# Eight, eight and six couples by seven products a layer: merged bank evacuation, in-place sums of weights, one ring of split pieces

## The chip, the cores and the metric

The kernel runs on one core of a Trainium2 chip. The metric is the device time of one execution in microseconds. Before the change the median of three runs was 2391.03 us (2389.68 to 2392.11).

## The reference

Two layers on 256 tokens of width 2048. A layer is RMSNorm, a token mixer (layer 0 an mLSTM, layer 1 an HGRN2), a residual, RMSNorm, a gated MLP with a depthwise convolution of width 3 along the tokens, and a residual; a last RMSNorm closes the trunk. The change touches mainly the MLP:

```
u = hn @ w_up                        # 2048 -> 2 x 5504
a, v = split(u)
c = conv_b + sum_j a[t + j - 1] * conv_w[j]
y = (gelu(c) * v) @ w_down           # 5504 -> 2048
```

## The kernel before

**Precision.** Every float32 operand x is used as two parts, a rounded high part (`wh`, made by ScalarE, L137) and the rest (`wl`, made by VectorE as x - wh, L138). A block product is three TensorE matmuls: high by high, high by low, low by high (`product`, L234). Each weight therefore passes through ScalarE and VectorE once. Weights come from HBM into `raw` tiles (three buffers of 128x2048) on the queue of SP, and the split *pieces* of 128x1024 go into a ring of four (`WB`).

**Chunks.** `stream` (L282) walks a list of chunks and stays three pieces ahead of TensorE (`LOOK`). An "fm" chunk gives one feature tile (up projections, queries, keys, gates), a "tm" chunk 512 output columns for the 256 tokens. An up chunk ("fm", `paced`) holds 128 columns of a and 128 of v. They fill two PSUM banks of `psm`; in each bank columns 0 to 255 hold the high sum and 256 to 511 the low one. `done_up` (in `ffn`, L1097 on) evacuates: copy the low half (ScalarE, L355), add (VectorE, L356), scale by the norm (L361), once for a and once for v; then the convolution (VectorE L1118 to L1120), Gelu, the product with v, and the split into the tile `g` (`GT`).

**Parts.** The MLP is done in two parts of 22 and 21 feature tiles. Part 0 is 22 up chunks, then two down *pairs* (output columns 0 to 1023, `w_d0`, and 1024 to 2047, `w_d1`). Part 1 is 21 up chunks, one pair (columns 0 to 1023) and two "tm" chunks for the rest.

**Pairs and couples.** A pair ("st", `squares_by_seven`, L226) takes two feature tiles (a *couple*) at a time, as a 2x2 by 2x2 block product: tokens are two blocks of 128, outputs two blocks of 512. A plain couple takes eight block products into the banks C11, C12, C21, C22 (tile `pc`). A couple listed in `SEVEN` takes seven (Winograd's form) with sums of the token blocks S1 to S4 and sums of the weight blocks T1 to T4, three of the products going into the banks P1, P5, P6, P7 (tile `mm`). `mid` adds these into the residual `hm` (VectorE and GpSimd, L547 to L554) after the last couple by seven, and `done` adds C11 to C22 (L559). In part 0 couples 1, 2, 4, 5, 7, 8, 9 and 1, 2, 4, 5, 7, 8 go by seven in the two pairs, in part 1 couples 1, 2, 4, 5, 7, 8: 19 a layer.

**Sums of weights.** Those of the couples in `STORED` (six a pair) are made while the up chunks run: `prepare` (L573) loads a couple's weights into tiles `pth`, three VectorE subtractions (L179, 182, 184) make the sums in `ptl`, and they go to HBM (`tscr`). `side.push` paces it: its waits are counted in units of TensorE work as emitted, 10.4 a chunk. The pair loads them back into tiles `T` (tag `avc`, three buffers, shared with the up chunks' evacuation). Couple 9 of the first pair makes its sums live. `combine` (L200) splits T into `th0`, `tl0`, `th1`, `tl1`, one buffer each (L209, L210). Sums of tokens are made in `token_sums` (L527) at the end of the odd up chunk.

**Mixers.** Their output projections (`mixed`, L587) hold one such pair of eight couples, three by seven, with sums made live.

**Order.** Instructions of an engine run in the order of a scheduler that plans when the program is built; it may move a matmul of one couple ahead of one of another. Waits are semaphores.

## Time and profile before

| what | value |
|---|---|
| median of three runs | 2391.03 us |
| span of the profiled execution | 2388.5 us (its whole time isn't given) |
| TensorE busy | 2372.4 us (99%), 14614 matmuls |
| VectorE busy | 1944.1 us (81%), 3221 instructions |
| ScalarE busy | 1298.8 us (54%), 2013 instructions |
| GpSimd busy | 189.7 us (8%) |
| moved by DMA | 555 MB, 232 GB/s over the span |

"Busy" of an engine is the time in which at least one of its instructions ran. A row of a group reads: line, engine, operation, output and inputs, shapes, count, then total busy time, mean time of one in ns, and the idle time before them with what ended it. A row of waits reads: who waited for whom, us in total, times, longest. A row of windows gives each engine's busy time in a stretch with its count, the granted clock of TensorE, the DMA engines' busy share and GB/s. A row of the chain or the timeline begins with its start and its length in us.

### The profile page before, as it was taken

Reading aid. Unit: us, or ns where it says so; the run is one execution under the profiler, and the core shown is the slowest. Engines: PE = TensorE matmul, PEld = TensorE weight load, DVE = VectorE, ACT = ScalarE, POOL = GpSimd, SP = SyncE. Lnnn points to the kernel's source line nnn. Section 1 sums busy time; section 2 is a strip of 40 time slices with the busy share of each in tenths; the row PEclk is TensorE's granted clock in tenths of the full one; section 3 lists DMA queues with packets and bytes.
Section 4 is the critical chain, followed back from the end, with each engine's and each line's share of the span. In section 5 each row is a group of like instructions: output and inputs, shape, how many; then the busy total and the mean of one; then the engine's idle time right before and its main releaser. Section 6 shows DMA issues by size and latency. Waiting matters only on the chain.

```text
span 2388.5 us, 37988 instructions
## 1 busy us (share of the span) xinstructions
PE 2372.4 (99%) x14614; PEld 2030.4 (85%) x14614; DVE 1944.1 (81%) x3221; ACT 1298.8 (54%) x2013; POOL 189.7 (8%) x240
## 2 busy tenths in 40 slices
PE   9999999999999999999999999999999999999998
PEld 7888888888888888888888888888888888888887
DVE  7766687988887888777888888888889888788874
ACT  7655455454564554555555555555555565454563
POOL 0100000000000000001222222220000000000000
PEclk9999999999999999999999999999999999999999
DMA  8654556988787777755554554545798888677774
GB/s 300 201 180 165 183 178 211 333 294 317 269 293 254 251 239 262 273 194 182 173 171 168 175 177 160 177 166 188 258 325 298 298 281 296 231 249 263 249 266 148
DMA packets 98789, 555.07 MB, mean 232 GB/s; under 512 B 11168, under 2 KB 11680, under 8 KB 50736
## 3 DMA queue, kind: packets, MB, share of 16 engines
q1 hardware_dynamic: 96912, 548.64, 65.6%
q0 software_dynamic: 1120, 3.21, 0.7%
q8 instruction: 114, 1.87, 0.3%
q10 hardware_dynamic: 576, 0.79, 0.1%
q14 instruction: 67, 0.55, 0.1%
HBM read 512.69 MB, written 39.91 MB: 231 GB/s over the span
## 4 chain that ended last, share of the span: by engine, by line
PE 98%; DVE 1%; issue 1%; DMA 0%; ACT 0%; SPq 0%; POOLq 0%; POOL 0%
PE mm L328 37%; PE mm L344 23%; PE mm L332 18%; PE pc L237 12%; PE mm L237 5%; PE pn L776 1%; PE py L1034 1%; PE pd L984 1%; PE pz L405 0%; PE pa L984 0%; DMA raw<-in_w_first 0%; PE S L762 0%; DVE tl L210 0%; PE pz L1055 0%; PE pa L1009 0%
## 5 line engine op out<-in xcount | busy, mean ns | idle before, releaser
L328 PE MATMUL mm<-xt,wh 128*128 128x512 f32 x3776 | 1313.4, 394 | 0.0
L137 ACT CAST wh<-raw 128x1024 fp32r<-128x1024 f32 (+1 forms) x846 | 853.5, 1019 | 693.8 <-PE mm L328 237.9
L138 DVE TENSOR_TENSOR wl<-raw,wh 128x1024 fp32r<-128x1024 f32 (+1 forms) x846 | 1004.7, 1195 | 265.1 <-ACT wh L137 257.6
L332 PE MATMUL mm<-xt,wl 128*128 128x256 f32 x3776 | 1045.9, 278 | 0.0
L328 PEld LDWEIGHTS mm<-xt,wh 128*128 128x128 f32 x3776 | 706.2, 188 | 159.4
L332 PEld LDWEIGHTS mm<-xt,wl 128*128 128x128 f32 x3776 | 709.5, 188 | 4.5 <-issue 0.4
L344 PE MATMUL mm<-wh,xt 128*128 128x512 f32 x1024 | 320.5, 391 | 3.0 <-ACT xt L350 1.3
L344 PEld LDWEIGHTS mm<-wh,xt 128*128 128x128 f32 x1024 | 191.4, 188 | 43.3 <-ACT xt L350 1.7
L344 PE MATMUL mm<-wl,xt 128*128 128x512 f32 x512 | 198.2, 391 | 0.0
L237 PE MATMUL pc<-wh,g 128*128 128x512 f32 x508 | 167.2, 389 | 0.0
L355 ACT COPY b<-mm 128x256 f32<-128x256 f32 x236 | 87.4, 370 | 122.9 <-PE mm L332 122.7
L210 DVE TENSOR_TENSOR tl<-T,th 128x1024 fp32r<-128x1024 f32 x88 | 109.9, 1264 | 38.9 <-ACT th L209 36.7
L209 ACT CAST th<-T 128x1024 fp32r<-128x1024 f32 x88 | 92.7, 1054 | 73.6 <-PE mm L237 43.5
L237 PEld LDWEIGHTS pc<-wh,g 128*128 128x128 f32 x508 | 95.4, 188 | 19.9
L344 PEld LDWEIGHTS mm<-wl,xt 128*128 128x128 f32 x512 | 96.2, 188 | 18.9
L553 POOL TENSOR_TENSOR hm<-hm,u 128x512 f32<-128x512 f32 x8 | 10.4, 1302 | 1150.9 <-DVE u L552 1150.9
L237 PE MATMUL pc<-wl,g 128*128 128x512 f32 x254 | 98.9, 389 | 0.0
L344 PE MATMUL mm<-wh,g 128*128 128x512 f32 x308 | 96.6, 392 | 0.0
L237 PE MATMUL mm<-th,sx 128*128 128x512 f32 x264 | 91.9, 390 | 0.0
L356 DVE TENSOR_TENSOR avc<-mm,b 128x256 f32<-128x256 f32 x172 | 72.0, 418 | 14.7 <-ACT b L355 14.7
L361 DVE TENSOR_TENSOR avc<-avc,R 128x256 f32<-128x256 f32 x172 | 71.9, 419 | 1.6
L976 DVE COPY kq<-QK 128x256 f32<-128x256 f32 x224 | 69.7, 336 | 0.0
(260 smaller groups left out, 2476.7 us busy)
## 6 DMA issues: line engine op xcount, KB each, us to landing
raw<-in_w_up SPq DMA_DIRECT2D x172, 1024.0 KB, 5.5
raw<-in_w_d SPq DMA_DIRECT2D x48, 1024.0 KB, 5.0
raw<-in_w_bq SPq DMA_DIRECT2D x48, 1024.0 KB, 4.9
pth<-in_w_d SPq DMA_DIRECT2D x72, 512.0 KB, 6.7
tscr<-ptl SPq DMA_DIRECT2D x72, 512.0 KB, 4.7
T<-tscr SPq DMA_DIRECT2D x72, 512.0 KB, 5.1
raw<-in_w_d SPq DMA_DIRECT2D x36, 768.0 KB, 5.2
raw<-in_w_ao SPq DMA_DIRECT2D x24, 1024.0 KB, 4.8
```

Of the source, the lines that this page charges most:

```text
L137: pin(act.copy(wh[:, :m], r))
L138: pin(dve.tensor_tensor(wl[:, :m], r, wh[:, :m].bitcast(F32), ALU.subtract))
L209: act.copy(th, t)
L210: dve.tensor_tensor(tl, t, th.bitcast(F32), ALU.subtract)
L237: pe.matmul(ps, a, b, start=id(ps) not in begun, stop=stop and i == 2)
L328: pe.matmul(ps[f], wh[:, c:c + P], x, start=k + kk == 0, stop=False)
L332: pe.matmul(ps[f][:, 0:T], wl[:, c:c + P], x[:, 0:T], start=False, stop=k + kk == ch.nk - 1)
L344: pe.matmul(ps[t], x[:, a + t * P:a + (t + 1) * P], w[:, c], start=st and i == 0, stop=sp and i == 2)
L355: act.copy(b, ps[:, T:2 * T])
L356: dve.tensor_tensor(dst, ps[:, 0:T], b, ALU.add)
L361: dve.tensor_tensor(dst, dst, R, ALU.mult)
L976: dve.tensor_copy(m[:, j].rearrange("k (m p j) -> k m p j", p=2, j=h), blocks(z, h, 0, T))
```

## The change

1. The two banks of a "fm" or "tm" chunk are one tile of two banks (`banks`, two buffers instead of four of one bank). An up chunk is evacuated by one copy, one addition and one scaling over both banks; the convolution's first term moves from VectorE to ScalarE.
2. All couples by seven of the MLP are stored: 8, 8 and 6 a layer, in part 0 couples 1 to 4 and 6 to 9 for both pairs. `prepare` subtracts in place, four subtractions of 512 columns, in tiles of the new ring's tags, and loads a couple one period ahead.
3. T2, T3, T4 come back in one tile `T` of 1536 columns and T1 into the tail of `raw`, so that T is split like raw weights, piece by piece. A couple by seven is four pieces: B11 and B22; T2 and T3; B21 and T1; T4. Every third piece of a pair uses two buffers in the stage's own pool, the others the ring of four.
4. The fourth token sum S4 lies in a half of a `g` tile that a couple by seven does not read (part 0), or in tiles of its own (part 1). Small tiles `b` and `gs` move to other pools.

```diff
 WB = 4
+MORE = 2
 MIX = 5
...
 GATES = 4 * AH
-SEVEN = (1, 2, 4, 5, 7, 8, 9), (1, 2, 4, 5, 7, 8), (1, 2, 4, 5, 7, 8)
-STORED = (1, 2, 4, 5, 7, 8)
+SEVEN = (1, 2, 3, 4, 6, 7, 8, 9), (1, 2, 4, 5, 7, 8)
 SCRATCH = 4096
...
     ev = ctx.enter_context(tc.tile_pool(name="ev", bufs=1))
-    psm = ctx.enter_context(tc.tile_pool(name="psm", bufs=4, space=PSUM))
+    psm = ctx.enter_context(tc.tile_pool(name="psm", bufs=2, space=PSUM))
     psa = ctx.enter_context(tc.tile_pool(name="psa", bufs=4, space=PSUM))
...
-        def parts(r, m, pin=lambda ins: ins):
-            wh = wpool.tile([P, 1024], F32R, tag="wh", bufs=WB, name="wh")
-            wl = wpool.tile([P, 1024], F32R, tag="wl", bufs=WB, name="wl")
+        def parts(r, m, pin=lambda ins: ins, more=None):
+            where, bufs = wpool, WB
+            if more is not None:
+                turns["w"] += 1
+                if turns["w"] % 3 == 0:
+                    where, bufs = more, MORE
+            wh, wl = (where.tile([P, 1024], F32R, tag=n, bufs=bufs, name=n) for n in ("wh", "wl"))
             pin(act.copy(wh[:, :m], r))
...
     def temporary(pool_, name):
-        return pool_.tile([P, 1024], F32, tag="avc", bufs=TEMP if pool_.name == "ff" else 2, name=name)
-    def weight_sums(a, b, T, T_):
-        B22, B21, B12 = a[:, 512:1024], b[:, 0:512], b[:, 512:1024]
-        dve.tensor_tensor(T.rearrange("p (a b) -> p a b", a=2), B12.unsqueeze(1).broadcast_to([P, 2, 512]),
-                          a.rearrange("p (a b) -> p a b", a=2), ALU.subtract)
-        yield 2.5
-        dve.tensor_tensor(T_[:, 0:512], B22, T[:, 0:512], ALU.subtract)
-        yield 2.5
-        dve.tensor_tensor(T_[:, 512:1024], B21, T_[:, 0:512], ALU.subtract)
+        return pool_.tile([P, 1536], F32, tag="avc", bufs=TEMP if pool_.name == "ff" else 2, name=name)
...
-        units, raws, kept, sums = (ch.nk + 1) // 2, {}, {}, {}
+        units, raws, kept = (ch.nk + 1) // 2, {}, {}
         side.until(lambda: ch.waits is None or ch.waits)
...
             if u not in raws and u < units:
-                raws[u] = load_raw(ch.src, 2048 * u, min(2048 * (u + 1), 1024 * ch.nk) - (512 if u in ch.stored else 0))
+                n = 1536 if u in ch.stored else min(2048, 1024 * ch.nk - 2048 * u)
+                raws[u] = load_raw(ch.src, 2048 * u, 2048 * u + n)
                 if u in ch.stored:
-                    kept[u] = [temporary(ch.pool, "T") for _ in range(2)]
-                    for t, src in zip(kept[u], ch.stored[u]):
-                        nc.sync.dma_start(t, src)
+                    kept[u] = temporary(ch.pool, "T")
+                    nc.sync.dma_start(kept[u], ch.stored[u][:, 0:1536])
+                    nc.sync.dma_start(raws[u][:, 1536:2048], ch.stored[u][:, 1536:2048])
             return raws.get(u)
...
         def combine(u):
-            r = raw(u)
-            T, T_ = kept[u] if u in kept else (temporary(ch.pool, "T") for _ in range(2))
-            if u not in kept:
-                for _ in weight_sums(r[:, 0:1024], r[:, 1024:2048], T, T_):
-                    pass
-            sums[u] = []
-            for i, t in enumerate((T, T_)):
-                th, tl = (ch.pool.tile([P, 1024], F32R, tag=n, name=n) for n in (f"th{i}", f"tl{i}"))
-                act.copy(th, t)
-                dve.tensor_tensor(tl, t, th.bitcast(F32), ALU.subtract)
-                sums[u].append((th, tl))
+            r, T = raw(u), temporary(ch.pool, "T")
+            B11, B22, B21, B12 = (r[:, j * 512:(j + 1) * 512] for j in range(4))
+            T2, T3, T4 = (T[:, j * 512:(j + 1) * 512] for j in range(3))
+            for x, y, out in ((B12, B22, T3), (B12, B11, B12), (B22, B12, T2), (B21, T2, T4)):
+                dve.tensor_tensor(out, x, y, ALU.subtract)
+            kept[u] = T
...
             r = raw(u)
-            if u + 1 in ch.seven and not ch.late:
+            yield *parts(r[:, 0:1024], 1024, more=ch.pool), 1
+            if u + 1 in ch.seven and u + 1 not in ch.stored:
                 combine(u + 1)
-            wh, wl = parts(r[:, 0:1024], 1024)
-            yield wh, wl, 1
-            if u + 1 in ch.seven and ch.late:
-                combine(u + 1)
+            if u in ch.seven:
+                yield *parts(kept[u][:, 0:1024], 1024, more=ch.pool), 1
             if 2 * u + 1 < ch.nk:
-                m = 512 if u in ch.seven else 1024
-                wh, wl = parts(r[:, 1024:1024 + m], m)
-                yield wh, wl, sums.pop(u, None)
+                yield *parts(r[:, 1024:2048], 1024, more=ch.pool), 1
+            if u in ch.seven:
+                yield *parts(kept[u][:, 1024:1536], 512, more=ch.pool), 1
+    def banks():
+        return psm.tile([P, 2, 512], F32, tag="mm", name="mm")
...
-        psm_ = [psm.tile([P, 512], F32, tag="mm", name="mm") for _ in range(4)]
-        P1, P6, P7, P5 = psm_
+        P1, P6, P7, P5 = psm_ = [ps[:, i] for ps in (banks(), banks()) for i in range(2)]
         C11, C12, C21, C22 = psa_ = [aux("pc") for _ in range(4)]
...
                 break
-            fetch()
-            q = ready.pop(0)
             x0, x1 = ch.x(2 * u), ch.x(2 * u + 1)
             A11, A21, A12, A22 = half(x0, 0), half(x0, 1), half(x1, 0), half(x1, 1)
-            B11, B22, B21 = block(p[:2], 0), block(p[:2], 1), block(q[:2], 0)
-            if u in ch.seven:
-                sx, t = ch.sums(u), q[2]
-                S1, S3, S2, S4 = ((sx[:, i * P:(i + 1) * P], sx[:, 512 + i * P:512 + (i + 1) * P]) for i in range(4))
-                T1, T3, T2, T4 = (block(t[i // 2], i % 2) for i in range(4))
-                for i, (ps, x, w) in enumerate(((P1, A11, B11), (C12, S4, B22), (C11, A12, B21), (P5, S1, T1),
-                                                (P7, S3, T3), (P6, S2, T2), (C21, A22, T4))):
+            def products(*them):
+                for ps, x, w in them:
                     product(ps, x, w, u == last and ps in psm_)
                     side.tick(0.65)
+            def piece():
+                fetch()
+                q = ready.pop(0)[:2]
+                return block(q, 0), block(q, 1)
+            B11, B22 = block(p[:2], 0), block(p[:2], 1)
+            if u in ch.seven:
+                S1, S3, S2, S4 = ch.sums(u)
+                products((P1, A11, B11), (C12, S4, B22))
+                T2, T3 = piece()
+                products((P6, S2, T2), (P7, S3, T3))
+                B21, T1 = piece()
+                products((C11, A12, B21), (P5, S1, T1))
+                T4, _ = piece()
+                products((C21, A22, T4))
                 if u == last:
...
                 continue
-            B12 = block(q[:2], 1)
+            B21, B12 = piece()
             for ps, (x, w), (y, v) in ((C11, (A11, B11), (A12, B21)), (C12, (A11, B12), (A12, B22)),
...
                     k += 1
-            ch.done(ps)
+            ch.done(both if ch.paced else ps)
...
-    def fm_sum(ps, dst):
-        b = ev.tile([P, T], F32, tag="b", bufs=3, name="b")
+    def fm_sum(mp, ps, dst):
+        b = mp.tile([P, T], F32, tag="b", bufs=3, name="b")
         act.copy(b, ps[:, T:2 * T])
...
-    def fm_scaled(ps, R, dst, scale=None):
-        fm_sum(ps, dst)
+    def fm_scaled(mp, ps, R, dst, scale=None):
+        fm_sum(mp, ps, dst)
         if scale is None:
...
-    def token_sums(mp, i, a, b, S):
-        sx = mp.tile([P, 1024], F32R, tag=f"sx{i}", name="sx")
+    def token_sums(mp, i, a, b, S, last=None):
+        m = 384 if last else 512
+        sx = mp.tile([P, 2 * m], F32R, tag=f"sx{i}", name="sx")
         for i, (x, y, op) in enumerate(((a[:, P:T], b[:, P:T], ALU.add), (a[:, P:T], a[:, 0:P], ALU.subtract),
...
             dve.tensor_tensor(S[:, i * P:(i + 1) * P], x, y, op)
-        act.copy(sx[:, 0:512], S)
-        dve.tensor_tensor(sx[:, 512:1024], S, sx[:, 0:512].bitcast(F32), ALU.subtract)
-        return sx
-    def pair(src, nk, c0, x, sums, norm, seven, late=False):
+        act.copy(sx[:, 0:m], S[:, 0:m])
+        dve.tensor_tensor(sx[:, m:2 * m], S[:, 0:m], sx[:, 0:m].bitcast(F32), ALU.subtract)
+        if last:
+            act.copy(last[0], S[:, m:512])
+            dve.tensor_tensor(last[1], S[:, m:512], last[0].bitcast(F32), ALU.subtract)
+        return [(sx[:, i * P:(i + 1) * P], sx[:, m + i * P:m + (i + 1) * P]) for i in range(m // P)] + ([last] if last else [])
+    def pair(src, nk, c0, x, sums, norm, seven):
...
         ch = Chunk("st", src, nk, x, done)
-        ch.mid, ch.seven, ch.sums, ch.late = mid, seven, sums, late
-        ch.stored, ch.waits = {}, None
+        ch.mid, ch.seven, ch.sums = mid, seven, sums
+        ch.stored, ch.waits, ch.pool = {}, None, None
         return ch
...
-        yield 24.0
-        for src, dst in todo:
-            r, T = ([mp.tile([P, 1024], F32, tag=f"{n}{i}", name=f"p{n}") for i in range(2)] for n in ("th", "tl"))
-            for i in range(2):
-                late(r[i], src[:, i * 1024:(i + 1) * 1024])
-            yield 9.0
-            yield from weight_sums(*r, *T)
-            for i in range(2):
-                nc.sync.dma_start(dst[i], T[i])
-            yield max(1.0, period - 14.0)
+        loaded = []
+        def load(i):
+            if i < len(todo):
+                n = ("wh", "wl")[i % 2]
+                r = [mp.tile([P, 1024], F32, tag=n, bufs=MORE, name=f"p{n}") for _ in range(2)]
+                for j in range(2):
+                    late(r[j], todo[i][0][:, j * 1024:(j + 1) * 1024])
+                loaded.append(r)
+        yield 18.0
+        load(0)
+        for i, (_, dst) in enumerate(todo):
+            yield period / 2
+            load(i + 1)
+            B11, B22, B21, B12 = (loaded[i][j // 2][:, j % 2 * 512:(j % 2 + 1) * 512] for j in range(4))
+            for x, y, out in ((B12, B22, B22), (B12, B11, B12), (B11, B22, B11), (B21, B11, B21)):
+                dve.tensor_tensor(out, x, y, ALU.subtract)
+                yield period / 8
+            for j in range(2):
+                nc.sync.dma_start(dst[:, j * 1024:(j + 1) * 1024], loaded[i][j])
         finished.append(True)
...
         stack = ExitStack()
-        box = dict(n=3 * len(STORED) * layer)
+        box = dict(n=(2 * len(SEVEN[0]) + len(SEVEN[1])) * layer)
         chunks, pairs = [], []
...
                 a, v, c = (avc[:, j * T:(j + 1) * T] for j in range(3))
-                fm_scaled(ps[0], R, a)
-                fm_scaled(ps[1], R, v)
+                av = avc[:, 0:2 * T].rearrange("p (a b) -> p a b", a=2)
+                act.copy(av, ps[:, :, T:2 * T])
+                dve.tensor_tensor(av, ps[:, :, 0:T], av, ALU.add)
+                dve.tensor_tensor(av, av, R.unsqueeze(1).broadcast_to([P, 2, T]), ALU.mult)
                 cw = [col("conv_w", (layer * 3 + w) * FT + f) for w in range(3)]
-                dve.tensor_scalar(c, a, cw[1], col("conv_b", layer * FT + f), ALU.mult, ALU.add)
+                act.activation(c, a, AF.Identity, bias=col("conv_b", layer * FT + f), scale=cw[1])
                 dve.scalar_tensor_tensor(c[:, 1:T], a[:, 0:T - 1], cw[0], c[:, 1:T], ALU.mult, ALU.add)
...
                 if i % 2 and i // 2 in seven:
-                    SX[i // 2] = token_sums(mp, seven.index(i // 2), box["c"], c, avc[:, 0:2 * T])
+                    n = seven.index(i // 2)
+                    if seven is SEVEN[0]:
+                        z = GT[i - 1][:, P:T], GT[i - 1][:, T + P:2 * T]
+                    else:
+                        if n % 3 == 0:
+                            box["s4"] = mp.tile([P, 768], F32R, tag=f"sx{len(seven) + n // 3}", name="s4")
+                        z = tuple(box["s4"][:, (n % 3 * 2 + j) * P:(n % 3 * 2 + j + 1) * P] for j in range(2))
+                    SX[i // 2] = token_sums(mp, n, box["c"], c, avc[:, 0:2 * T], z)
                 box["c"] = c
...
                     begin()
-                side.push(prepare(box["mp"], todo, (nf * 10.4 - 24.0) / len(todo) - 1.5, finished))
+                side.push(prepare(box["mp"], todo, (nf * 10.4 - 26.0) / len(todo), finished))
             for i in range(nf):
-                chunks.append(Chunk("fm", w_up[layer, f0 + i], KT, norm.x, done_up(f0 + i, i, GT, SX, SEVEN[2 * part]),
+                chunks.append(Chunk("fm", w_up[layer, f0 + i], KT, norm.x, done_up(f0 + i, i, GT, SX, SEVEN[part]),
                                     prep if i == 0 else None,
...
                 ch = pair(src, nf, c0, lambda k: GT[k], lambda u: SX[u], norm, seven)
-                for u in STORED:
+                for u in seven:
                     ch.stored[u] = tscr[box["n"]]
...
-            chunks.append(two(w_d0[layer][:, f0 * 1024:(f0 + nf) * 1024], 0, nxt if part else None, SEVEN[2 * part]))
+            chunks.append(two(w_d0[layer][:, f0 * 1024:(f0 + nf) * 1024], 0, nxt if part else None, SEVEN[part]))
             if part:
...
             else:
-                chunks.append(two(w_d1[layer], 2, None, SEVEN[1]))
+                chunks.append(two(w_d1[layer], 2, None, SEVEN[0]))
         return chunks, stack.close
...
     mscr = nc.dram_tensor("mscr", (64, T), F32, kind="Internal").ap()
-    tscr = nc.dram_tensor("tscr", (6 * len(STORED), 2, P, 1024), F32, kind="Internal").ap()
+    tscr = nc.dram_tensor("tscr", (4 * len(SEVEN[0]) + 2 * len(SEVEN[1]), P, 2048), F32, kind="Internal").ap()
     with tile.TileContext(nc, schedule_with_timeline_sim=True) as tc:
...
```

14 lines of the change are left out of this document (8 added, 6 removed).

## The prediction

> **What bounds the kernel now.** I read the page first, then the waits of TensorE, then the chain of waits in the down stages, then busy time by stage.
>
> ```profile
> span 2388.5 us, 37988 instructions
> PE 2372.4 (99%) x14614; PEld 2030.4 (85%) x14614; DVE 1944.1 (81%) x3221; ACT 1298.8 (54%) x2013; POOL 189.7 (8%) x240
> PE 98%; DVE 1%; issue 1%; DMA 0%; ACT 0%; SPq 0%; POOLq 0%; POOL 0%
> ```
> ```profile
> PE pd L984 <- issue: 2.6, 2, 1.4
> PE mm L344 <- ACT xt L350: 1.3, 1, 1.3
> PE idle L1171 <- POOL ones L1164: 1.1, 1, 1.1
> PE mm L344 <- issue: 0.9, 1, 0.9
> PE mm L344 <- ACT wh L137: 0.8, 1, 0.8
> PE mm L237 <- DVE tl L210: 0.6, 2, 0.3
> ```
> ```profile
> 739.06 8.16 PE pc L237 x36
> ```
> ```profile
> core 0: us, PE busy (x) PEld busy (x) DVE busy (x) ACT busy (x) POOL busy (x), PEclk, DMA share, GB/s
> 590.00:600.00 10.00, 10.00 (x60) 8.73 (x59) 9.05 (x16) 4.79 (x8) 0.00 (x0) 1.00 1.00 379
> 392.20:635.60 243.40, 243.40 (x1409) 212.88 (x1408) 213.57 (x360) 126.71 (x190) 0.70 (x1) 1.00 0.82 296
> 635.60:690.00 54.40, 54.40 (x242) 45.03 (x241) 43.80 (x51) 33.25 (x39) 0.00 (x0) 1.00 0.84 295
> 690.00:745.00 55.00, 54.70 (x241) 44.74 (x240) 45.39 (x46) 31.46 (x34) 7.08 (x4) 1.00 0.77 272
> ```
>
> TensorE is the bound throughout: 98% of the chain, all its listed waits together 7.3 us. In a down pair 36 products take 8.16 us, so one 128x512 product costs 0.2267 us. The clock is 1.00 in every stage row. So what the change wins is TensorE work removed, and what it can lose is new TensorE idle time. The window rows are layer 0's up chunks of part 0 (22 chunks, 11.06 us each), its first down pair and its second. VectorE has 12% to spare in the ups and 17 to 20% in the pairs. The DMA engines stand at shares 0.77 to 0.84.
>
> **The change, part by part.** *TensorE.* Couples done by seven products go from 7+6+6 to 8+8+6 a layer, three more in each of two layers. A couple costs 8 block products of three matmuls, or 7: each saves three. 6 x 3 x 0.2267 = 4.08 us. The built programs agree: 18 fewer 128x512 matmuls, no other count on TensorE changed. This is the only term with a sure sign.
>
> *VectorE and ScalarE in the ups.*
>
> ```profile
> L138 DVE TENSOR_TENSOR wl<-raw,wh 128x1024 fp32r<-128x1024 f32 x782 | 963.8, 1237 | 257.0 <-ACT wh L137 249.6
> L210 DVE TENSOR_TENSOR tl<-T,th 128x1024 fp32r<-128x1024 f32 x88 | 109.9, 1264 | 38.9 <-ACT th L209 36.7
> L356 DVE TENSOR_TENSOR avc<-mm,b 128x256 f32<-128x256 f32 x172 | 72.0, 418 | 14.7 <-ACT b L355 14.7
> L361 DVE TENSOR_TENSOR avc<-avc,R 128x256 f32<-128x256 f32 x172 | 71.9, 419 | 1.6
> L179 DVE TENSOR_TENSOR ptl<-pth 128x1024 f32<-128x1024 f32 x36 | 44.0, 1223 | 26.5 <-DMA pth<-in_w_d 22.7 <-issue 3.6
> L138 DVE TENSOR_TENSOR wl<-raw,wh 128x512 fp32r<-128x512 f32 x64 | 43.9, 686 | 8.1 <-ACT wh L137 8.1
> L1118 DVE TENSOR_SCALAR avc<-avc,pp 128x256 f32<-128x256 f32 x86 | 34.9, 406 | 0.0
> L532 DVE TENSOR_TENSOR avc<-avc 128x128 f32<-128x128 f32 x104 | 30.0, 288 | 2.0
> L182 DVE TENSOR_TENSOR ptl<-pth,ptl 128x512 f32<-128x512 f32 x36 | 24.6, 683 | 0.0
> L534 DVE TENSOR_TENSOR sx<-avc,sx 128x512 fp32r<-128x512 f32 x26 | 17.8, 684 | 0.0
> ```
> ```profile
> L137 ACT CAST wh<-raw 128x1024 fp32r<-128x1024 f32 x782 | 817.5, 1052 | 676.9 <-PE mm L328 237.9 <-PE mm L344 156.6 <-issue 151.5
> L355 ACT COPY b<-mm 128x256 f32<-128x256 f32 x236 | 87.4, 370 | 122.9 <-PE mm L332 122.7
> L1121 ACT ACTIVATE avc<-avc 128x256 f32<-128x256 f32 x86 | 35.7, 415 | 42.3 <-DVE avc L1120 42.1
> L546 ACT COPY u<-mm 128x512 f32<-128x512 f32 x8 | 4.7, 585 | 0.1
> ```
>
> A chunk's evacuation on VectorE was 2x418 + 2x419 + 406 = 2080 ns. Now it is two 512-wide operations at about 684, as the conv's first term goes to ScalarE: 1368, so 0.71 us less a chunk, 15.7 us less in part 0. An operation over two banks is in no row; its bounds are 684 (as one bank) and 2x418 (nothing won), and I take 684 because rows of 128x512 read PSUM at that price. In part 0 the stored couples go from 12 to 16, each 4x683 = 2.73 us in place of 1223 + 2x683 = 2.59: 43.7 against 31.1, +12.6. Token sums go from 7 couples at 4x288 + 684 = 1.84 to 8 at 4x288 + about 0.55 (384 wide, between 288 and 684) + 0.29 = 1.99: +3.0. Sum: 15.6 more, 15.7 less; VectorE stays at about 214 of 243 us. ScalarE per chunk: 585 + 415 in place of 2x370, +0.26 us, 5.7 us on 127 of 243. The extra hop (VectorE waits for ScalarE's first conv term, ScalarE for VectorE's product) holds up the splits queued behind it on both engines by up to about 0.4 us a chunk (one operation of 406 or 415 ns); the weight pieces are split up to four pieces of 2.77 us ahead, so I cost it at nothing. Without that cover it would be 86 x 0.4 = 34 us.
>
> *Merged banks.* The two banks of a chunk come free together, but the next user is two chunks on, 11 us later: nothing. The mixer stages get the same pair of banks and new places for small tiles: no operation added; I take 0, bounds -1 and +1 (one of the issue waits of 0.9 or 1.4 us more or less).
>
> *The ring of six in the pairs.* A couple by seven on VectorE was 1237 + 2x1264 + 686 = 4.45 us and is 3x1237 + 686 = 4.40, under 21 x 0.2267 = 4.76 of TensorE; a plain couple is 2.47 under 5.44. Both part-0 pairs now hold 8x4.40 + 3x2.47 + 10 additions of about 0.68 = 49.4 us. The first pair of before held 7x4.45 + 4x2.47 + 2.59 (sums made live) + 6.8 = 50.4 and the second 45.9. So the new pairs are no denser than the first pair, which ran at full rate. What that pair lost comes at its end:
>
> ```profile
> 676.05 2.36 DVE L210 TENSOR_TENSOR tl<-T,th 128x1024 fp32r<-128x1024 f32 x2
> 694.50 4.27 DVE L210 TENSOR_TENSOR tl<-T,th 128x1024 fp32r<-128x1024 f32 x2
> ```
> ```profile
> 694.16 1.30 POOL L553 TENSOR_TENSOR hm<-hm,u 128x512 f32<-128x512 f32 x1 [300.17 <-DVE u L552]
> 695.41 2.29 POOL L554 TENSOR_TENSOR hm<-hm,u 128x512 f32<-128x512 f32 x1
> ```
> ```profile
> 698.14 0.39 PE L237 MATMUL mm<-th,sx 128*128 128x512 f32 x1
> 698.83 0.50 PE L237 MATMUL mm<-tl,sx 128*128 128x512 f32 x1 [0.30 <-DVE tl L210]
> ```
>
> Two splits take 4.27 us instead of 2.36 while GpSimd adds, and TensorE's next start comes 0.69 us after the last one, 0.46 late; two such waits stand in the table. The Trainium skill (SBUF — State Buffer, "Who interferes with whom" and "SBUF: two separate sides") says that a VectorE operation with two SBUF inputs and a GpSimd operation exclude each other for a whole instruction. By that rule, with which the rows agree, splits against these additions pay again, and the merged evacuations, which read PSUM, would not. The additions and their place stay, so the 0.46 us (about the same in layer 1) stays: between 0 (hidden) and the 1.9 us of the slowed splits, twice. I take no change.
>
> *Queue of SP and DMA.*
>
> ```profile
> pth<-in_w_d SPq DMA_DIRECT2D x72, 512.0 KB, 6.7
> tscr<-ptl SPq DMA_DIRECT2D x72, 512.0 KB, 4.7
> T<-tscr SPq DMA_DIRECT2D x72, 512.0 KB, 5.1
> raw<-in_w_d SPq DMA_DIRECT2D x36, 768.0 KB, 5.2
> ```
> ```profile
> 621.65 3.32 SPq L197 DMA_DIRECT2D T<-tscr  x2
> ```
>
> Eight more stored couples (36 to 44): each adds 1 MB read and 1 MB written in the ups. SP issues 675 to 723 DMAs. In part 0's ups that is 4 x 2.1 MB in 243.4 us, 34 GB/s more: 296 becomes 330, share 0.82 becomes about 0.92. A couple by seven loads 768 + 2x512 = 1792 KB in both versions, a plain one 1024; a part-0 pair now moves 8x1792 + 3x1024 KB = 17.8 MB in 8x4.76 + 3x5.44 = 54.4 us, 328 GB/s against 295 and 272. The 10 us at 379 show that it fits; I cost it at nothing, and this is the cover that I trust least.
>
> Sum: 2388.5 - 4.1 = 2384.4 of span. No whole time of the profiled execution is given; the median of the runs, 2391.0, lies 2.5 above its span, and I carry that: **2387.0 us**.
>
> **The rivals.** *The loads limit the pairs (slower).* Place: the four part-0 pairs, above all their two runs of four couples by seven, which ask 1792 KB per 4.76 us, 385 GB/s. Before, T of couple 1 was asked for at 621.65, 14 us ahead of the stage. In the built order it stands on SP behind the load of couple 3, which waits for a raw buffer of couple 0. If the gaps between issues keep the rate near 305 (share 0.87), a pair takes 17.8 / 0.305 = 58.4 us, +4.0, four times: 2387 + 16 = 2403; it decides below about 322 GB/s, where four pairs lose the 4.1 us. For it: shares 0.82 to 0.84 already. Against it: three raw buffers ahead, and 379 seen. The Trainium skill (DMA: Bandwidth & Descriptors, "Specifications") puts the HBM share of a core at about 358 GB/s; as an estimate by it, a run of four would fall 1.4 us short, eight times 11 us if nothing were ahead. The 379 lies above that figure, so the measurement decides against it as a ceiling here.
>
> *The gain leaks at the seams (no change).* The last stored couples are subtracted shortly before the ups end, and VectorE has waited up to 22.7 us in all for such loads (L179's row). From the order, T of couple 1 goes out some 3 us before the pair, lands 5.2 later, is split by 1052 + 1237 ns: ready at +4.5, wanted after 33 products, +7.5. If VectorE is 5 us late there, TensorE loses 2 us a layer: 2391.
>
> *More than the products.* Both 0.46 us waits vanish and an issue wait goes: 2387.0 - 0.9 - 0.9 = 2385.2.
>
> **How the numbers follow.** The forecast (2386.0 to 2388.5) gets 0.42, the loads 0.23 (2395 to 2405), the seams 0.18 (2388.5 to 2393), more than the products 0.17. A measurement here tells about 0.2%, 4.8 us, from no change, so faster means under 2386.3: 0.17 and a third of the forecast's share less noise, 0.31. Slower means over 2395.8: 0.22. Same: 0.47. The range runs from 2384.3 (more than the products, with 0.9 of spread) to 2400 (inside the loads' case), leaving out about 0.16; the forecast's own is 2386.0 to 2388.5.
>
> **What would show it.** TensorE count down by 18; its waits still near 7 us; the evacuation rows at 128x512 near 0.68 on VectorE and 0.59 on ScalarE; part-0 pairs of 54.4 us at a DMA share near 0.93. The forecast is wrong if TensorE waits on a split of T or raw in runs of couples 1 to 4 or 6 to 9, if a pair is longer than 56 us, or if an operation over two banks costs as much as two.

## The result and the profile after

The changed kernel takes 2399.57 us (median of nine runs, 2393.55 to 2401.02) against 2391.03 us before on the same chip: ratio 1.0033, 95% interval 1.0025 to 1.0041. It is slower by 0.33%; the forecast was 2387.0 us. By these medians it is 8.5 us longer; the profiled execution, from which the stages are read, is 10.3 us longer in span than the one of before (2398.8 against 2388.5).

The page of the kernel after, its span, busy times and chain:

```profile
span 2398.8 us, 38064 instructions
PE 2376.2 (99%) x14596; PEld 2031.0 (85%) x14596; DVE 1935.9 (81%) x3081; ACT 1352.4 (56%) x2055; POOL 190.8 (8%) x240
PE 91%; DMA 4%; DVE 3%; issue 1%; ACT 0%; SPq 0%; POOL 0%; POOLq 0%; DVEq 0%; ACTq 0%
```

TensorE has 18 matmuls less and still is busy 3.8 us longer; the chain is no longer TensorE's alone. Its waits (who waited for whom, us in total, times, longest):

```profile
PE pd L1002 <- issue: 5.9, 3, 2.3
PE pc L229 <- ACT wh L142: 2.8, 4, 1.7
PE mm L229 <- ACT wh L142: 1.3, 1, 1.3
PE pc L229 <- DVE wl L143: 0.8, 1, 0.8
PE mm L315 <- DVE hm L484: 0.8, 1, 0.8
```

Where they lie is told by the starts of the stages, read from the first matmul of each in TensorE's timeline and set against before. The table gives how much longer (+) or shorter a stage is than before, in us, for the kernel after and the experiments told below; each column is one profiled execution.

| stage | after | e1 | e4 | e6 | e8 | e5 | e11 | e12 | e14 |
|---|---|---|---|---|---|---|---|---|---|
| layer 0 up to its FFN | +0.9 | -1.6 | -0.5 | 0.0 | -0.4 | -1.0 | -0.3 | -1.0 | 0.0 |
| FFN 0, ups of part 0 | 0.0 | 0.0 | 0.0 | 0.0 | 0.0 | 0.0 | 0.0 | 0.0 | +4.2 |
| FFN 0, two pairs | +1.1 | +0.5 | -0.8 | 0.0 | -2.6 | -2.1 | +0.8 | +2.5 | -0.5 |
| FFN 0, rest | 0.0 | 0.0 | 0.0 | 0.0 | 0.0 | 0.0 | 0.0 | 0.0 | 0.0 |
| HGRN up to its output pair | +5.4 | -4.0 | +4.1 | -4.1 | -4.0 | -4.0 | -3.3 | -4.0 | -4.2 |
| output pair and chunk after it | +4.7 | +5.6 | +4.7 | 0.0 | +5.0 | +4.0 | -0.5 | +3.5 | +0.7 |
| FFN 1, ups of part 0 | 0.0 | 0.0 | 0.0 | 0.0 | 0.0 | 0.0 | +0.5 | 0.0 | +4.2 |
| FFN 1, two pairs | -2.5 | 0.0 | -2.6 | +0.7 | -2.7 | -2.7 | -0.5 | +4.1 | -2.8 |
| FFN 1, rest and end | +0.8 | +0.8 | +0.8 | 0.0 | +0.7 | +0.8 | 0.0 | +0.8 | 0.0 |
| span against 2388.5 | +10.3 | +1.2 | +5.7 | -3.5 | -4.0 | -5.0 | -3.4 | +5.8 | +1.7 |

The first row moves by a microsecond from run to run (e4 has the same instructions there as after), and is left aside. The pairs here are the two down pairs of part 0. FFN 1's won what the products promise, FFN 0's lost it again. The two largest rows, +5.4 and +4.7, stand in HGRN and its output pair, in a mixer whose arithmetic the change does not touch. The pairs themselves, in windows of the kernel after (FFN 0's two, then FFN 1's two), and its evacuation rows:

```profile
636.30:692.30 56.00, 53.67 (x235) 43.18 (x234) 49.54 (x59) 39.87 (x50) 0.00 (x0) 1.00 0.95 360
692.30:748.90 56.60, 56.59 (x249) 46.34 (x248) 49.34 (x52) 34.07 (x38) 3.52 (x2) 1.00 0.81 290
1937.00:1991.50 54.50, 54.50 (x243) 45.09 (x241) 48.34 (x56) 38.70 (x48) 0.00 (x0) 1.00 0.96 369
1991.50:2046.00 54.50, 54.50 (x241) 44.93 (x240) 47.74 (x50) 34.16 (x39) 3.53 (x2) 1.00 0.80 289
```
```profile
L1136 DVE TENSOR_TENSOR avc<-avc,R 128x512 f32<-128x512 f32 x86 | 59.0, 686 | 1.0
L1135 DVE TENSOR_TENSOR avc<-mm,avc 128x512 f32<-128x512 f32 x86 | 58.7, 683 | 0.1
L1138 ACT ACTIVATE avc<-avc,pp 128x256 f32<-128x256 f32 x86 | 51.7, 601 | 35.6 <-DVE avc L1136 35.0
L1134 ACT COPY avc<-mm 128x512 f32<-128x512 f32 x86 | 49.9, 580 | 0.0
```

A pair without stalls takes 54.5 us, FFN 1's first at 369 GB/s and its second at 289. In its window FFN 0's first lost 2.3 us of TensorE; it ends at 694.07, 57.8 us after its first matmul, so the prediction's sign of being wrong, a pair longer than 56 us, came true there. An addition over two banks costs 683 ns, as taken. In HGRN three waits on "issue" follow bursts of short matmuls, and after two of them TensorE's clock falls:

```profile
1232.61 0.31 PE L1002 MATMUL pd<-kq 128*32 128x32 f32 x10 [1.79 <-issue]
1357.90 0.27 PE L1002 MATMUL pd<-kq 128*32 128x32 f32 x9 [1.80 <-issue]
1485.06 0.33 PE L1002 MATMUL pd<-kq 128*32 128x32 f32 x6 [2.35 <-issue]
```
```profile
1232.60:1236.60 4.00, 3.99 (x31) 3.48 (x32) 2.67 (x8) 2.96 (x8) 1.08 (x2) 1.00 0.54 223
1358.00:1362.00 4.00, 4.00 (x22) 3.42 (x22) 1.85 (x8) 2.36 (x6) 1.07 (x2) 0.57 0.55 225
1485.00:1489.00 4.00, 3.94 (x20) 3.39 (x21) 1.37 (x6) 1.35 (x3) 1.07 (x2) 0.60 0.48 199
```

The column before the last two is the granted clock, 0.57 and 0.60 on the mean of 4 us. Inside these windows it is 0.50 for 3.41 us:

```profile
1358.46:1361.86 3.40, 3.40 (x13) 2.91 (x12) 1.44 (x7) 1.76 (x5) 1.07 (x2) 0.50 0.53 217
```

There a pair of matmuls takes 0.64 us in place of 0.35. Before, three such waits summed to 3.5 us, at other bursts, with the clock at 1.00. Now they sum to 5.9, and the two stretches at half speed cost 1.6 us each: 5.6 worked out, 5.4 measured. In e3 and e4 below, with waits at the same three bursts but half speed behind two and behind one of them, HGRN is 6.1 and 4.1 us longer than before.

### The profile page after: what moved, and what is told of

It reads as the page before. It is cut to its first block, busy times and chain, and to the rows that moved or that the text cites. A ratio compares the mean times of both kernels' runs of the same rounds, so it can differ in the third digit from the quotient of the medians.

```text
span 2398.8 us, 38064 instructions
## 1 busy us (share of the span) xinstructions
PE 2376.2 (99%) x14596; PEld 2031.0 (85%) x14596; DVE 1935.9 (81%) x3081; ACT 1352.4 (56%) x2055; POOL 190.8 (8%) x240
## 3 DMA queue, kind: packets, MB, share of 16 engines
q8 instruction: 114, 1.87, 0.3%
## 4 chain that ended last, share of the span: by engine, by line
PE 91%; DMA 4%; DVE 3%; issue 1%; ACT 0%; SPq 0%; POOL 0%; POOLq 0%; DVEq 0%; ACTq 0%
PE mm L331 33%; PE mm L347 22%; PE mm L335 17%; PE pc L229 10%; PE mm L229 5%; DMA pwl<-in_w_d 1%; DVE wl L143 1%; DMA pwh<-in_w_d 1%; DMA tscr<-pwl 1%; PE pn L794 1%; PE py L1052 1%; PE pd L1002 1%; PE pz L408 0%; PE pa L1002 0%; DMA Mb<-mscr 0%
## 5 line engine op out<-in xcount | busy, mean ns | idle before, releaser
L142 ACT CAST wh<-raw 128x1024 fp32r<-128x1024 f32 (+1 forms) x846 | 875.5, 1040 | 763.9 <-PE mm L331 446.6
L143 DVE TENSOR_TENSOR wl<-raw,wh 128x1024 fp32r<-128x1024 f32 (+1 forms) x846 | 1033.3, 1227 | 332.8 <-ACT wh L142 330.3
L229 PE MATMUL pc<-wh,g 128*128 128x512 f32 x576 | 196.4, 390 | 0.0
L229 PE MATMUL pc<-wl,g 128*128 128x512 f32 x288 | 112.3, 390 | 0.8 <-DVE wl L143 0.8
L143 DVE TENSOR_TENSOR wl<-T,wh 128x1024 fp32r<-128x1024 f32 (+1 forms) x100 | 95.3, 962 | 20.3 <-ACT wh L142 19.8
L229 PE MATMUL mm<-wh,sx 128*128 128x512 f32 x300 | 108.0, 390 | 1.3 <-ACT wh L142 1.3
L142 ACT CAST wh<-T 128x1024 fp32r<-128x1024 f32 (+1 forms) x100 | 82.5, 835 | 45.0 <-PE pc L229 25.8
L599 DVE TENSOR_TENSOR pwl<-pwl 128x512 f32<-128x512 f32 x88 | 60.3, 685 | 14.9 <-DMA pwl<-in_w_d 14.7
L1138 ACT ACTIVATE avc<-avc,pp 128x256 f32<-128x256 f32 x86 | 51.7, 601 | 35.6 <-DVE avc L1136 35.0
L599 DVE TENSOR_TENSOR pwh<-pwh 128x512 f32<-128x512 f32 x88 | 60.2, 685 | 11.5 <-DMA pwh<-in_w_d 6.3
```

Source lines behind the costliest of these rows:

```text
L142: pin(act.copy(wh[:, :m], r))
L143: pin(dve.tensor_tensor(wl[:, :m], r, wh[:, :m].bitcast(F32), ALU.subtract))
L229: pe.matmul(ps, a, b, start=id(ps) not in begun, stop=stop and i == 2)
L599: dve.tensor_tensor(out, x, y, ALU.subtract)
L1138: act.activation(c, a, AF.Identity, bias=col("conv_b", layer * FT + f), scale=cw[1])
```

## The experiments

Each line of times is against the kernel before on the same chip (ratio with its 95% interval).

**HGRN: where the packets of instructions end.** One queue of the profile after carries TensorE's instructions, as its size tells:

```profile
q8 instruction: 114, 1.87, 0.3%
```

114 packets of 1.87 MB in all are 16 KB each; shared over 14596 matmuls and as many weight loads that is 64 bytes an instruction, so a packet holds 128 matmuls with their loads. A burst of HGRN is 128 matmuls of 32 or 64 columns; ahead of the first wait 118 of them were through in 1.3 us (the expectation below has 0.5). In windows of 0.2 us one packet comes at 1230.2, 1355.6 and 1482.6 us, beside the three waits, and TensorE goes on some 2.3 us after it. The window 1230.2 to 1230.4:

```profile
q8 instruction: 1, 0.02, 30.8%
```

Two kernels move the bursts against the packets' ends by the number of idle matmuls, which keep TensorE busy at the program's start (each counts as two; they are made wider by as much):

```diff
-    for i in range(90):
+    for i in range(51):        # e1_idle51; 75 in e2_idle75
```

> Theory (instruction pages): TensorE's instructions come in packets of 16 KB, 256 instructions, 128 matmuls with their weight loads; HGRN's bursts of 128 matmuls of 32 rows and columns use up one packet in 0.5 us where a burst lies nearly whole in one packet, and TensorE then stands until the next has come. 51 idle matmuls at the start in place of 90 (each counts as two; wider, so that the idle stretch lasts as long) move every burst by 78 of 128 against the packets' ends, to places where no burst lies nearly whole in one. Expected: the three issue waits at the bursts (1.79, 1.80, 2.35 us) all under 0.5, no granted clock under 0.9 in 1340:1500, HGRN 6 us shorter; span near 2393, time near 2393.5. Rival (the waits belong to these bursts, by the work before them or by DMA traffic at that time): three waits of 1.8 to 2.4 us stay at the same bursts, span near 2398.8.

> Theory (instruction pages): 75 idle matmuls in place of 90 move the bursts by 30 of 128 the other way, so that the bursts that began 36, 35 and 33 after a packet's end (at about 1211, 1336, 1463 and 1590 us) now begin 3 to 6 after one, and the ones that waited begin 20 before. Expected: issue waits of 1 to 2.4 us move to three or four of the bursts at 1211, 1336, 1463, 1590, and those at 1230, 1355, 1482 wait under 0.5; span between 2395 and 2401. Rival (the waits belong to their bursts): they stay at 1230, 1355 and 1482.

e1: 2390.84 us, 1.0003 (0.9994 to 1.0013). HGRN is 9.4 us shorter than in the kernel after (6 were expected). No wait on issue is left, and the clock is 1.00 over all of HGRN:

```profile
1093.00:1605.00 512.00, 512.00 (x4665) 441.62 (x4664) 445.24 (x915) 284.07 (x546) 141.46 (x177) 1.00 0.50 173
```

e2 (two runs): 2414.89 us, 1.0104 (1.0084 to 1.0125). The waits have moved to the four bursts named, but are longer than expected:

```profile
1213.83 0.33 PE L1002 MATMUL pd<-kq 128*32 128x32 f32 x5 [3.78 <-issue]
1343.60 0.32 PE L1002 MATMUL pd<-kq 128*32 128x32 f32 x3 [3.65 <-issue]
1473.67 0.27 PE L1002 MATMUL pd<-kq 128*32 128x32 f32 x2 [3.95 <-issue]
1603.15 0.79 PE L347 MATMUL mm<-wh,xt 128*128 128x512 f32 x1 [3.75 <-issue]
```
```profile
1214.00:1218.00 4.00, 4.00 (x14) 3.17 (x12) 3.44 (x15) 0.00 (x0) 0.00 (x0) 0.50 0.41 170
```

At the first of them the packet comes at 1211.2, 1.2 us after TensorE has run out of work, and at each of them the clock falls to half. The theory holds, its rival falls: 15 idle matmuls less cost 15 us, 39 less win 9. The same was then done to the kernel before.

```diff
-    for i in range(90):
+    for i in range(65):        # in the kernel before
```

> The kernel before with 65 wider idle matmuls in place of 90, and nothing else: every burst moves by 50 of 128 against the ends of the instruction packets. Theory (instruction packets): its own three issue waits (1.24, 1.38, 0.87) go, the last burst may wait instead; HGRN 2.5 to 4 us shorter, time near 2387.5. Rival: the waits stay, time 2391.

2387.16 us, 0.9988 (0.9979 to 0.9997), HGRN 4.1 us shorter: the kernel before had its own share of these waits. Between the two kernels without a long one (e1 and e6) the change costs 3.7 us.

**FFN's seams: the preparation ends too late.** The seam is the border between the up chunks and the first pair. In the kernel after ScalarE's splits for the first pair wait for the stores of the preparation, whose tiles are the places of the ring that the pair needs; T of couple 1 is then asked for at 638.61, behind the loads of raw:

```profile
630.16 2.00 ACT L142 CAST wh<-raw 128x1024 fp32r<-128x1024 f32 x2 [5.68 <-DMA tscr<-pwh]
635.75 2.00 ACT L142 CAST wh<-raw 128x1024 fp32r<-128x1024 f32 x2 [0.96 <-DMA tscr<-pwl]
638.61 0.38 SPq L192 DMA_DIRECT2D T<-tscr  x1
638.17 0.50 PE L229 MATMUL pc<-wl,g 128*128 128x512 f32 x1 [0.81 <-DVE wl L143]
646.32 0.73 PE L229 MATMUL mm<-wh,sx 128*128 128x512 f32 x2 [1.28 <-ACT wh L142]
```
```diff
-                side.push(prepare(box["mp"], todo, (nf * 10.4 - 26.0) / len(todo), finished))
+                side.push(prepare(box["mp"], todo, (nf * 10.4 - 46.0) / len(todo), finished))
```

> Theory (the preparation ends too late): the last stored couples are loaded, subtracted and stored in the two ring places that the pair's first pieces need; the last store lands at 635.7, and ScalarE and VectorE wait for it (5.68, 0.96, 0.27 us), which makes the first pieces, the raw buffers and the loads of T late. A preparation planned to end 20 us earlier in each part frees the places before the pair. Expected: the waits on splits at 636.7, 644.7 and 646.9 (0.99, 1.43, 0.46 us late) shrink to under 0.5 in sum, FFN 0 2 to 2.9 us shorter, FFN 1 unchanged; span near 2396.3. Rival (T is late because its load stands on SP behind the load of couple 3): T of couple 1 is still asked for at about 638.6 and TensorE still waits 1.4 us for its split; span within 1 us of 2398.8.

2396.06 us, 1.0027 (1.0017 to 1.0036). T is asked for 7.4 us earlier (6.0 us against the pair's start), and one wait of 0.66 us is left at the seam:

```profile
631.17 0.38 SPq L192 DMA_DIRECT2D T<-tscr  x1
```

FFN 0's pairs gain 1.9 us: the theory holds, and the rival, by which T would still be asked for at 638.6, falls. With the idle matmuls of e1 beside it (e8_both):

> 51 idle matmuls and the early preparation, and nothing done to the mixers. Theory: the gain of the two adds up: HGRN 4 us shorter than before, its output pair 5 us longer, FFN 0's pairs 1 us and FFN 1's 2.5 us shorter; span near 2387, time near 2388 to 2389. Rival (the early preparation moves the instruction stream or crowds the up stages): less than 1 us better than e1_idle51, time 2390 to 2391.

2386.06 us, 0.9984 (0.9975 to 0.9993): both FFNs' pairs now win 2.6 and 2.7 us, the 2.04 us of nine matmuls less and the 0.4 to 0.5 us wait at the pairs' border, which is gone. Without the early preparation the seam differed from run to run with the same instructions in it: FFN 1's pairs gave -2.5 us in the kernel after and 0.0 in e1.

**The products.** Six couples by seven in every pair:

```diff
-SEVEN = (1, 2, 3, 4, 6, 7, 8, 9), (1, 2, 4, 5, 7, 8)
+SEVEN = (1, 2, 4, 5, 7, 8), (1, 2, 4, 5, 7, 8)
```

> The changed kernel with six couples in every pair (18 a layer in place of 22) and 45 idle matmuls, so that the bursts of HGRN lie as with 51 idle matmuls in the kernel e1_idle51. Theory (the products are worth their full time, and neither loads nor splits bound a pair in its middle): against e1_idle51 each part-0 pair is 2 x 0.68 = 1.36 us longer, FFN 0 and FFN 1 2.7 us each, apart from the seam; span near 2395. Rival (loads or splits bound the pairs with eight couples): the pairs with six are no longer or even shorter, span 2390 or less.

(In it the fourth token sums of part 1 lie in tiles that are still in use, so that part is computed from other values; the work is the same.) 2395.6 us, 1.0019 (1.0009 to 1.0030). Against e1, the comparison set in advance, FFN 0's pairs are 0.3 us shorter, which is the rival's sign: e1 loses 3.0 us at the seam, and this kernel, with four couples fewer to prepare, nothing. Against e8, which loses nothing there either, each of FFN 0's pairs takes 1.36 us more, 2.7 in all, four couples at 0.68 us: the products are worth their full time, and nothing else bounds a pair's middle. FFN 1's are 6.8 longer than e8's, 2.7 by products and 2.7 by two waits on a late T (2.25 and 0.44); the rest isn't explained.

**HGRN's output pair.** In the kernel after, couple 4's and couple 6's additions stand mixed on VectorE, eight in a run, and TensorE waits 1.69 us for a split behind them. First theory: their order.

```diff
-            r, T = raw(u), temporary(ch.pool, "T")
+            r = raw(u)
+            T = temporary(ch.pool, "T") if ch.pool.name == "ff" else ch.pool.tile([P, 1536], F32, tag="T", name="T")
...
-                f = temporary(two.pool, "f")
+                f = two.pool.tile([P, 1024], F32, tag="avc", name="f")
```

> Theory (VectorE's order in HGRN's output pair): the additions of couple 6 stand among those of couple 4 on VectorE, because two temporaries are free, eight operations of 0.6 us in one run at 1642.5 to 1648; ScalarE's splits of the raw half and of T wait for them, and TensorE for those. With one T buffer beside one for the tokens' sums, couple 6's additions come after couple 4's splits. Expected: TensorE's waits of 1.69, 0.45, 0.44 us at 1643 to 1650 go; the pair from 1618.9 on is 3 to 4 us shorter; span near 2395.3. Rival (the ring of pieces or the additions in place, not their order, limit the pair): waits of 2 us or more stay there in sum, span near 2398.8.

2401.25 us, 1.0047 (1.0032 to 1.0062), the pair 5.2 us longer than before. The wait of 1.69 us went, and another came at the pair's end, where the next chunk needs both banks of a pair of banks:

```profile
PE mm L348 <- DVE u L556: 2.4, 1, 2.4
```

e5_pin also keeps the first three additions of `mid` in program order (`pin(dve.tensor_tensor(...))`), with the remedies of e8:

> All remedies together: 51 idle matmuls, the early preparation, one T buffer in the mixers, and the first three additions of a pair's end on VectorE kept in the order of the program, so that the pair of banks P1 and P6 is free first. Theory (three separate causes: instruction packets, VectorE's order in HGRN's output pair, the late end of the preparation): HGRN 4 us shorter than before, its output pair within 2 us of before's, FFN 0's pairs 1 to 2 and FFN 1's 2.5 us shorter than before's; span near 2383, time near 2386, faster than the kernel before by about 4 us. Rival (the output pair is limited by VectorE's amount of work, whatever its order): 3 us or more stay lost there, span 2387 or more.

2385.36 us, 0.9982 (0.9972 to 0.9992), the fastest of all versions. On the same chip e6, the kernel before with other idle matmuls alone, took 2387.16, so only 1.8 of the 4.9 us won come with the change and its remedies. Of the pair's 5 us 4.0 stay, as its rival said. Second theory: the sums are wanted too early in a couple.

```diff
...
+                B21, T1 = piece()
+                products((C11, A12, B21), (P5, S1, T1))
                 T2, T3 = piece()
                 products((P6, S2, T2), (P7, S3, T3))
-                B21, T1 = piece()
-                products((C11, A12, B21), (P5, S1, T1))
```

> The changed kernel with 51 idle matmuls (as e1_idle51) and the order of a couple's pieces and products swapped in all pairs: B21 with T1 second, T2 with T3 third, so that the sums are wanted after 12 matmuls of the couple (2.7 us) in place of 6 (1.4 us). Theory (the changed kernel wants the sums too early in a couple; the wait of a stored T at the seam and of the live sums in HGRN's output pair is this 1.36 us): against e1_idle51 the wait on T at the seam of FFN 0 (1.28 us) falls under 0.3 and the output pair of HGRN gets 1 to 2.5 us shorter, the run of eight additions on VectorE staying; span 2386 to 2388. Rival (the order of products does not matter, VectorE's order alone does): output pair and seams within 0.7 us of e1_idle51, span 2389 to 2390.

> The kernel e5_pin (all remedies) with the same swap. Theory: of the 4.0 us that e5_pin still loses against the kernel before in HGRN's output pair, the three waits on splits of sums (0.23, 0.37, 0.34 us, with the uneven matmuls after them 2 us in sum) go, the wait of 1.20 us for the next chunk's first split may stay; output pair 2 us shorter, span near 2381.5, time near 2383.5. Rival: the pair stays 4 us long over before's, span 2383.5.

e9: 2390.09 us, 1.0002 (0.9992 to 1.0011); e10: 2388.28 us, 0.9991 (0.9982 to 1.0000). The pair stays 5.4 and 6.4 us too long, so this theory falls too (at FFN 0's seam the wait did halve, 1.28 to 0.60).

Part of these figures is the clock. In e1, e8, e9 and e10 half speed lies in the pair or the chunk behind it for 3.41 us, in the kernel after and in e3, e4 and e5 it does not; by half of its length it can cost up to 1.7 us. In e1:

```profile
1633.16 0.50 PE L229 MATMUL pc<-wh,yb 128*128 128x512 f32 x1 [1.69 <-ACT wh L142]
1635.70:1639.00 3.30, 3.15 (x8) 1.85 (x7) 3.30 (x5) 2.37 (x3) 0.00 (x0) 0.50 0.75 263
```

In the kernels without it the loss is still 4.0 to 5.2 us. A loss that comes back elsewhere whatever wait is taken away suggests that the pair starts with a debt. It shows ahead of it. The kernel after, TensorE's last two transposes of HGRN's outputs (the pair starts at 1618.87) and what VectorE does next:

```profile
1618.84 0.27 PE L1073 MATMUL pz<-cst,y 128*128 128x128 f32 x1
1622.85 0.27 PE L1073 MATMUL pz<-cst,y 128*128 128x128 f32 x1
1623.16 0.69 DVE L201 TENSOR_TENSOR T<-raw 128x512 f32<-128x512 f32 x1 [3.17 <-PE pz L1073]
1645.60 0.49 PE L229 MATMUL pc<-wh,yb 128*128 128x512 f32 x1 [1.69 <-ACT wh L142]
```

The same of the kernel before, whose pair starts at 1611.55:

```profile
1610.17 0.38 PE L1055 MATMUL pz<-cst,y 128*128 128x128 f32 x2
1610.59 1.22 DVE L179 TENSOR_TENSOR T<-raw 128x1024 f32<-128x1024 f32 x1 [0.86 <-PE pz L1055]
```

The first live sum came 1.0 us ahead of the pair before and comes 4.3 us behind its start now; VectorE, 45 of 50 us busy there, cannot make that up. Third theory: the pairs of banks moved the work of HGRN's last head, whose transposes these are. One kernel takes them out of the changed kernel, one puts them alone into the kernel before.

```diff
-    psm = ctx.enter_context(tc.tile_pool(name="psm", bufs=2, space=PSUM))
+    psm = ctx.enter_context(tc.tile_pool(name="psm", bufs=4, space=PSUM))
...
-        return psm.tile([P, 2, 512], F32, tag="mm", name="mm")
+        return [psm.tile([P, 512], F32, tag="mm", name="mm") for _ in range(2)]
...
-                act.copy(av, ps[:, :, T:2 * T])
-                dve.tensor_tensor(av, ps[:, :, 0:T], av, ALU.add)
+                for x, s in zip((a, v), ps):
+                    act.copy(x, s[:, T:2 * T])
+                    dve.tensor_tensor(x, s[:, 0:T], x, ALU.add)
```

> The changed kernel with four single banks in place of two pairs of banks (the evacuation takes two ScalarE copies and two VectorE additions again; the product with R and the first term of the conv stay as changed), the early preparation, and 70 idle matmuls, which put the bursts where e6_before65 has them. Theory (the pair of banks moves the end of HGRN's last head: in the built order its last two transposes stand 1 ahead of and 17 matmuls inside the output pair, where the kernel before has them 7 and 6 ahead of it; the pool of HGRN closes only after them, so the live sums start late and VectorE has no slack in that pair): with single banks the order is that of before, and the output pair costs what it cost there (within 0.7 us, against 4 to 5 us more in the runs so far); HGRN 4 us and each FFN's pairs 2.5 us shorter than before; span near 2380, time near 2382.5. Rival (the ring and the sums in place cost the output pair its 4 us): pair 4 us longer than before, span near 2384.

> The kernel before with one part of the change alone: pairs of banks and the evacuation of both at once (46 idle matmuls, which put the bursts of HGRN where e1_idle51 has them). Theory: the output pair of HGRN is 4 to 5 us longer than before's with nothing else changed; HGRN 4 us shorter by the packets; FFN stages as before; span near 2388.5 to 2389.5. Rival (the pair of banks does nothing, the ring does): output pair as before, span near 2384.5.

e11: 2387.71 us, 0.9986 (0.9977 to 0.9995), its output pair 0.5 us shorter than before's. e12: 2397.51 us, 1.0027 (1.0017 to 1.0036), its pair 3.5 us longer. Transposes and first sum in e11 (pair from 1608.72), then in e12 (pair from 1608.95):

```profile
1607.35 0.38 PE L1073 MATMUL pz<-cst,y 128*128 128x128 f32 x2
1607.77 0.69 DVE L201 TENSOR_TENSOR T<-raw 128x512 f32<-128x512 f32 x1 [0.86 <-PE pz L1073]
```
```profile
1612.93 0.27 PE L1056 MATMUL pz<-cst,y 128*128 128x128 f32 x1
1613.24 1.23 DVE L179 TENSOR_TENSOR T<-raw 128x1024 f32<-128x1024 f32 x1 [3.17 <-PE pz L1056]
```

The order of the kernel before comes back without pairs of banks, and the order after comes with them alone, to the same wait of 3.17 us. The idle matmuls, which differ too, do not do it: with pairs of banks the pair is 3.5 to 6.4 us longer with 90, 75, 51, 46 or 45 of them, and the kernel before keeps its pair with 65 (e6). That settles the place; why the scheduler moves the head stays open. Alone, in the kernel before, the pairs of banks cost 3.5 us; the kernel after loses 4.7. In e12 FFN 0's pairs also lost 2.5 us, to waits for banks that come free two at a time (1.53 and 1.17 us at 691 to 693), and FFN 1's 4.1, to two waits at the same place (1.69 and 0.98) and half speed behind them. In e11 FFN 0's pairs took 3.4 us and FFN 1's 2.2 more than in e8, so its FFN gain was missed although the preparation is early: T is asked for 2.1 us ahead of FFN 0's pair, in e8 5.3. Why is open.

**Putting it together.**

> e11_single with one T buffer in the mixers and the first additions of a pair's end kept in the order of the program. Theory: little is left to mend in the output pair once its sums start early; span within 1.5 us of e11_single, near 2380.

> The changed kernel with pairs of banks in the FFN stages only (the pool of banks is closed and opened again between mixer and FFN, single banks in the mixers), the early preparation and 70 idle matmuls. Theory (each cause as found: packets in HGRN, pairs of banks in its output pair, the late preparation at the FFN's seams): HGRN 4 us shorter than before, its output pair within 0.7 us of before's, both FFNs' pairs 2.5 us shorter; the new pool may cost up to 1 us at each of four stage borders; span 2379 to 2383, time 2381.5 to 2385.5, faster than all before it. Rival (the merged evacuation in the FFN alone already moves the mixers' order, through the planner): output pair 3 us or more longer than before, span 2384 or more.

e13 (e11 with the edits of e3 and e5): 2392.78 us, 1.0008 (1.0000 to 1.0017). e14 opens the pool of banks anew at each border between mixer and FFN, pairs of banks in the FFN only: 2391.63 us, 1.0004 (0.9995 to 1.0013). In e14 HGRN, its output pair and FFN 1's pairs came as forecast (table), FFN 0's gained only 0.5. Its rival falls: merged evacuation and pairs of banks in the FFN alone, with single banks in the mixers, leave the output pair within 0.7 us of before. What spoilt both, with spans of 2390.5 and 2390.2 us where 2380 and 2379 to 2383 were expected, is something else. In the up chunks of some stages (layer 0's in e13, part 0's of both layers in e14) the matmuls came more slowly; e13, then e11, in the same window:

```profile
390.00:636.00 246.00, 246.00 (x1400) 213.52 (x1399) 214.52 (x352) 138.44 (x218) 0.70 (x1) 1.00 0.89 320
390.00:636.00 246.00, 246.00 (x1424) 215.19 (x1423) 213.89 (x354) 137.66 (x218) 0.70 (x1) 1.00 0.89 322
```

100 matmuls of up chunks take 17.67 us in these stages and 17.33 in the up stages of every other kernel here, evenly from the stage's start to its end, without a wait and at a clock of 1.00; 4.2 to 4.4 us a stage. Its cause stays open. Without it e14 would stand 8.4 us lower, near 2383; that is worked out, not run.

## Why the prediction was wrong

*TensorE, -4.08 us.* Right: 14596 matmuls, and e8 and e7 show the 2.04 us a layer and the 0.68 us a couple. The 2.5 us carried from span to time was 1.8 in the profiled execution (2400.6 against 2398.8).

*VectorE and ScalarE in the ups, 0.* Right in sum. Additions and scalings took 683 and 686 ns, the copy 580. The conv's first term took 601 ns on ScalarE, not 415 as Gelu's row had let me take, and it was hidden: no up stage changed by more than 0.04 us in the kernel after.

*Merged banks, "the mixer stages get the same pair of banks and new places for small tiles: no operation added; I take 0, bounds -1 and +1".* This is the step that failed. No operation was added, but the order was changed: the last transposes moved into the output pair, which was 4.7 us longer (the pairs of banks alone cost 3.5 in e12; taking them out gave back 5.2 in e11). In HGRN the waits on issue, which I had taken for fixed events to be counted one more or less, depend on where every instruction stands in its packet: +5.4 us (e1, e2). That is 10.1 us of the 10.3. Which edit moved the packets' ends was not isolated: the nine matmuls fewer ahead of HGRN do, and other instructions in the stream may. That it cost time here was luck in so far as the kernel before had waits of 3.5 us of its own, and a shift of the stream took them from each of the two (e1, e6). Another 0.8 us at the end comes with the pairs of banks too (the wait for hm L484 is there in e12 and not in e11).

*Ring of six, no denser.* Right. "The 0.46 us stays" was wrong: it went in both layers, as the rival "more than the products" had it.

*Queue and DMA, 0.* Right for FFN 1's pairs: 54.4 to 54.6 us, at 369 GB/s in the first and 289 in the second (329 on average against the 328 worked out), and with the early preparation FFN 0's come to the same (e8), so the rival that the loads limit the pairs falls. In the ups 320 GB/s and 0.89 against 330 and 0.92. At the seam wrong: with 2.5 us to win, FFN 0's pairs ended 1.1 us longer, 3.6 us lost. "The gain leaks at the seams" named T of couple 1 and, for a T 5 us late, a loss of 2 us a layer; T was asked for 2.3 us behind the pair's start in place of 3 ahead, TensorE waited for its split (1.28 us at 646.32, one of the prediction's signs of being wrong), and FFN 0 lost 3.6, FFN 1 nothing. It did not name what made T late, the ring's places in the hands of the preparation.

The 0.22 for slower rested on the loads; the kernel was slower by two mechanisms to which I had given no chance.

## What to carry to other kernels

A change of tiles in one stage can move the planned order in every stage that shares the pool: compare the order of all stages, and look ahead of each stage for the last work of the one before it. Where bursts of very short matmuls run, a small saving can be outweighed by where the instruction packets end; shift the stream by a few idle instructions, in the old kernel as in the new, before judging a change by a few microseconds. A loss that keeps its size while its waits move can be a late start: see when the stage's first operand was ready.

## What was not expected of the hardware

- TensorE's instructions arrive 256 at a time, and a burst of 128 short matmuls can outrun them: waits of 0.9 to 4.0 us, each ending 2.2 to 2.7 us after a packet.
- The granted clock fell to 0.50 for 3.41 us at a time, in e2 for 6.83. The length of the wait alone did not decide it: in e4 a wait of 1.99 us had half speed behind it and one of 2.14 had not, and the same wait of 1.69 us in the output pair had it in e1 and not in the kernel after.
- The Trainium skill (TensorE: Matmul & The Clock Gate, "What's actually happening") puts the fall to half speed after an idle window of about 3.4 us. Here it came sooner, with waits of 1.69 to 2.35 us and, in e2, 2.6 to 2.8 us into waits of 3.7 to 4.0; the measurement decides.
- The pace of the up chunks has two values, 17.33 and 17.67 us for 100 matmuls, and keeps one through an up stage.
